# Expert weights of a mixture-of-experts layer: split whole chunks ahead of use, in a ring of three

## The chip, the cores and the metric

One core of one Trainium2 chip runs the kernel. The metric is device microseconds of one execution; lower is better. All operands in memory are fp32.

## The reference

The model is a two-layer trunk on 256 latent and 256 context tokens, width 1024: in each layer a mixer (mLSTM, neighbourhood attention, latent attention), then a feed-forward part. That of layer 0 is a dense SwiGLU, that of layer 1 sends each of the 256 latent tokens to the two best of 8 experts. The change touches only this last part:

```python
def swiglu(x, w1, w3, w2): return (silu(x @ w1) * (x @ w3)) @ w2
h = modulate(rmsnorm(x, norm2_w), shift, scale)
y = moe_ffn(h, router_w, moe_w1, moe_w3, moe_w2)   # top 2 of 8, gates from a softmax
x = x + gate * y
return rmsnorm(x, final_norm_w)
```

w1 and w3 of an expert are 1024 x 2816, w2 is 2816 x 1024: 34.6 MB for an expert, 277 MB for all eight.

## The kernel before, in words

**Places.** `stage_two` sorts the experts by how many tokens they have and works through them in that order, one *place* (`e`, 0 to 7) after another, in `experts(rank, "a")`. Which expert stands at a place is known only on the chip; the numbers are loaded into registers of the queue engine SP (line 1287) and used as offsets of the weight loads. Places 1, 3 and 5 are *narrow* (64 slots for tokens), the others *wide* (128 slots). Tokens beyond a place's slots go through a second call, `experts(rk2, "b")`, behind a branch; it is not taken here.

**Precision.** PE multiplies in fp32r, a shortened fp32 that it streams faster than fp32. To keep fp32's accuracy, an operand is split into a high part (a cast to fp32r) and a low part (the value less the high part). A wide place makes three matmuls for each weight tile (lines 1277 to 1279: high x high, high x low, low x high). A narrow place puts the high and low parts of its 64 slots side by side in 128 columns and makes two (`narrow`, lines 1078 and 1079); the rows of the low half are then added to those of the high half by a last matmul, the *fold* (line 1283), which reads a copy of the bank that ACT has made (line 1282, `aev`).

**A place.** The h phase has 11 blocks `b`, each 512 columns of the joined w1 and w3, in two chunks (`kh`) of 128 x 2048 fp32 (1 MB): 22 chunks. After each block come silu on ACT (line 1298), the multiply on DVE (line 1299, tile `as`), two transposes on PE (line 1302, `atr`), and the high and low part of the result (narrow: `agh`, lines 1309 and 1310; wide: `agh`, `agl`, lines 1314 and 1315). The y phase has 11 chunks of w2, from which two banks of 512 columns are summed, each evicted with the gate (lines 1352 and 1353, `ayy`) and scattered to the tokens (lines 1361 and 1365, `asc` and `x`); the scatter of the second half is done within the next place.

**The split.** `wsplit` (line 1048) loads a chunk on SP's queue into one of 9 raw buffers (`NQ` + `NX`; at chunks 13 and 14, `SP0`, two more buffers that are free by then), casts each 1024-column half on ACT (line 1064) and subtracts it on DVE (line 1065). The halves lie in a ring of `NSW` = 4, that is two chunks. It is called in the text where the chunk is used. In a narrow place five of the 33 chunks (`WHOLE`) are not split: PE multiplies them as fp32 (line 1076). The names in a trace: `am_0w`, `am_1w` are the raw chunks of the two `kh`, `av_0w` to `av_10w` those of w2; `wh` and `wl` are the split halves.

**The order.** Nothing writes the order of instructions out: a scheduler places what the text traces, by a model of its own, and each engine then runs its list.

**Place 0** holds extra work: `order` (line 1286) computes the sort of the experts in some 25 small DVE instructions, and `place` (line 1290) builds the marks `G` of places 1 to 7, two DVE instructions each (line 1139), all after blocks 2 and 3.

The program prints `order`, `wsplit` and the rest below. In it, `nm` is `"a"`, `P` is 128, `NF` is 22, `KT` is 8, `NFB` is 11.

Of the kernel before, what the change touches and what calls it, by code (L numbers as in the profile page):

```python
# [18 lines left out]
P = 128  # L19
D = 1024  # L20
KT = 8
# [9 lines left out]
NQ, NX = 1, 8  # L31
# [7 lines left out]
SP0 = 13  # L39
BK = 7  # L40
# [5 lines left out]
NSW = 4  # L46
# [12 lines left out]
WHOLE = (3, 10, 16, 23, 29)  # L59
T_R, T_M0, T_M1, T_UP, T_LO, T_BO, T_K = 0, 512, 896, 1280, 1408, 1536, 1664  # L60
# [10 lines left out]
def trunk(ctx: ExitStack, tc: tile.TileContext, I, out):  # L71
# [952 lines left out]
    def stage_two(s2):  # L1024
# [5 lines left out]
        nchunk = [0]  # L1030

# [7 lines left out]
        def raws(k, name):  # L1039
            if k < SP0 or k >= SP0 + len(SPEC):  # L1040
                rp, rb, rtag = (wq, NQ, "raw") if k % (NQ + NX) < NQ else (wp, NX, "rawx")
                return [rp.tile([P, 2048], F32, tag=rtag, bufs=rb, name=name)]
            where = SPEC[k - SP0]
            if where == "x1":
                return [whole.tile([P, 2048], F32, tag="x1", name=name)]
            return [wq.tile([P, 2048], F32, tag="big", name=name)]

        def wsplit(src, name, split=True):
            rt_ = raws(nchunk[0], name + "w")
            w = 2048 // len(rt_)  # L1050
            for i, raw in enumerate(rt_):
                nc.sync.dma_start(raw, src[:, i * w:i * w + w])
            nchunk[0] += 1
            if not split:
                return [(rt_[0][:, :1024], None), (rt_[0][:, 1024:], None)]
            res = []
            for j in range(2):
                h = wp.tile([P, 1024], F32R, tag="wh", bufs=NSW, name=f"{name}wh{j}")
                l = wp.tile([P, 1024], F32R, tag="wl", bufs=NSW, name=f"{name}wl{j}")
                step = 512 if nchunk[0] <= NFINE or nchunk[0] > NCHUNK - NFINE2 else 1024  # L1060
                for i in range(0, 1024, step):
                    c, o = slice(i, i + step), j * 1024 + i
                    r = rt_[o // w][:, o % w:o % w + step]
                    act.copy(h[:, c], r)  # L1064
                    dve.tensor_tensor(l[:, c], r, f32(h[:, c]), op=OP.subtract)  # L1065
                res.append((h, l))
            return res


        def unit(ws, k, c0=0, n=512):  # L1070
            return [t if t is None else t[:, k % 2 * 512 + c0:k % 2 * 512 + c0 + n] for t in ws[k // 2]]
# [93 lines left out]
        def order():  # L1165
# [4 lines left out]
            oi = tile_([P, NEXP + 1], "oi", dt=I32)  # L1170
            hot = w[:, 192:256].rearrange("p (a b) -> p a b", a=NEXP)
# [11 lines left out]
            dve.tensor_tensor(hot, pos[:, None, :].to_broadcast(sq8), row[2][:, :, None].to_broadcast(sq8), op=OP.is_equal)  # L1183
            dve.tensor_tensor(w1_, hot, i8[:, None, :].to_broadcast(sq8), op=OP.mult)
            dve.tensor_reduce(idx, w1_, AX.X, OP.add)
            dve.tensor_copy(oi[:, :NEXP], idx)
            f4 = [P, 2, NEXP, NEXP]
# [5 lines left out]
            for dst, src in ((rankp, rank), (asgp, asg), (gatep, gate)):  # L1193
                by_place(dst, src)
            dve.tensor_tensor(w1_, hot, cnt[:, None, :].to_broadcast(sq8), op=OP.mult)
# [6 lines left out]
            fold = whole.tile([P, P], F32R, tag="before", name="fold")  # L1202
            dve.tensor_copy(fold[:, :64], ident[:, 64:])
            dve.tensor_scalar(fold[:, 64:], ident[:, :64], 0.0, None, op0=OP.mult)
            return oi, fold
# [3 lines left out]
        def experts(rk, nm):  # L1209
# [3 lines left out]
            late = []  # L1213

# [43 lines left out]

            for e in range(NEXP):
# [3 lines left out]
                slim = e in thin  # L1263
                n_ = 64 if slim else P
                gts = []
                for b in range(NFB):
                    p = bank("h", 2, f"{nm}h{e}_{b}")
                    for kh in range(2):
                        ws = wsplit(weights("m13", e, b, kh), f"{nm}m{e}_{b}_{kh}", not (slim and 2 * b + kh in WHOLE))
                        for k4 in range(4):  # L1270
# [3 lines left out]
                            if slim:  # L1274
                                narrow(p, xh, (wH, wL), kt == 0, kt == KT - 1)
                                continue
# [3 lines left out]
                    if slim:  # L1280
                        ev = cp.tile([P, 512], F32, tag="pm", bufs=3, name=f"{nm}ev{e}_{b}").bitcast(F32R)
                        act.copy(ev, p)
                        pe.matmul(p, oi[1], ev, start=False, stop=True, skip_group_check=True)
                    if nm == "a" and e == 0 and b == SLB:
                        gates()
                        oi.extend(order())
                        regs.extend([0] + [nc.values_load(oi[0][0:1, s_:s_ + 1], engines=[mybir.EngineType.SP], min_val=0,
                                                          max_val=NEXP - 1) for s_ in range(1, NEXP)])
                    if nm == "a" and e == 0 and b == SLB + 1:
                        place(rankp, asgp, 1, NEXP, nm)  # L1290
                    if b == SLB + 1:
                        slots(e)
# [4 lines left out]
                    s = cp.tile([P, 512], F32, tag="pm", bufs=3, name=f"{nm}s{e}_{b}")[:n_, :256]  # L1297
                    act.activation(s, p[:n_, :256], AF.Silu)  # L1298
                    dve.tensor_tensor(s, s, p[:n_, 256:], op=OP.mult)  # L1299
                    tr = bank("t", 2, f"{nm}tr{e}_{b}")  # L1300
                    for u in range(2):
                        pe.transpose(tr[:, u * n_:(u + 1) * n_], s[:, u * P:(u + 1) * P], ident[:n_, :n_])
                    if b % 4 == 0:
                        gh4 = w1.tile([P, 8, P], F32R, tag="raw", bufs=NRAW, name=f"{nm}gh{e}_{b}")
                        gl4 = None if slim else w1.tile([P, 8, P], F32R, tag="wh", bufs=NSP, name=f"{nm}gl{e}_{b}")
                    gh = gh4[:, 2 * (b % 4):2 * (b % 4) + 2, :]
                    trv = tr[:, :2 * n_].rearrange("p (u s) -> p u s", u=2)
                    if slim:
# [10 lines left out]
                for u in range(2 * NF):  # L1319
# [3 lines left out]
                    if u % 4 == 0:  # L1323
                        ws = wsplit(weights("m2", e, u // 4), f"{nm}v{e}_{u // 4}", not (slim and 22 + u // 4 in WHOLE))
                    if e == NEXP - 1 and u == NF:
                        pm = bank("h", 2, nm + "fpm")
                        xw = cp.tile([P, KT, NL], F32, tag="h", bufs=4, name=nm + "xw")
                    if f == 0:
                        y = bank("y", 2, f"{nm}y{e}{hh}")

                    end = e == NEXP - 1 and hh == 1
                    if end and f == 0:
                        ys = [y, bank("h", 2, f"{nm}y{e}{hh}b")]
# [4 lines left out]
                    for q in range(512 // n):  # L1338
                        yq = ys[q][:, :n] if end else y
                        for u_ in units:  # L1340
                            f = u_ % NF
                            wH, wL = unit(ws, u_ % 4, q * n, n)
                            if slim:
                                narrow(yq, gts[f // 2][0][:, f % 2, :], (wH, wL), f == 0, f == NF - 1)
                                continue
# [202 lines left out]
```

## Time and profile before

| | before |
|---|---|
| median of 3 runs | 1828.65 us (1827.77 to 1829.8) |
| profiled execution | 1828.04 us |
| its span, first to last instruction | 1826.2 us |
| mean granted TensorE clock | 0.983 |
| up to the first matmul of place 0 | 1023.2 us |
| places 0 to 7 | 1023.2 to 1807.1 us |
| last scatter, final norm, output | 1807.1 to 1826.2 us |

A place is cut here at its first h matmul and its first y matmul. The eight take 108.0, 82.9, 101.5, 95.9, 101.5, 95.9, 100.6 and 97.6 us in order. Engines: PE is the matrix engine, PEld its weight loads, DVE the vector engine, ACT the scalar engine, SP the queue that issues weight loads. "ah L1079 <- DVE am_1wl L1065" reads: the instruction of line 1079 that writes tile `ah` waited for DVE's instruction of line 1065 that writes `am_1wl`. "xN" is a count of instructions. Busy times of neighbours on an engine can overlap a little, since an instruction starts before the one ahead of it has ended.

### The profile page before, as it was taken

What the parts mean: (1) busy time and instruction counts of PE and PEld (TensorE: products, weight loads), DVE (VectorE), ACT (ScalarE), POOL (GpSimd) and SP (SyncE); (2) the same over time, 40 slices, a digit from 0 to 9 for tenths busy, and PEclk for the clock granted to TensorE, in tenths of its full rate; (3) what the DMA queues carried; (4) which work ended last, traced back from release to release, by engine and by line L of the source; (5) the groups of instructions that cost most, each with busy time, mean ns of one, the idle gap of its engine ahead of it and who ended that gap; (6) DMA issues with size and microseconds to landing.
All of it is one profiled execution on the core that took longest, in us unless ns stands there. A gap on an engine that the chain in (4) does not pass through costs nothing.

```text
span 1826.2 us, 24297 instructions
## 1 busy us (share of the span) xinstructions
PE 1754.1 (96%) x8594; PEld 1333.9 (73%) x8594; DVE 1376.5 (75%) x2460; ACT 1037.5 (57%) x1661; POOL 3.0 (0%) x9
## 2 busy tenths in 40 slices
PE   6999999999999999899999899999999999999997
PEld 4776766778888888687768777678756875578886
DVE  4667757679986333577767799898968897798996
ACT  3455556533222222365466578877767776777784
POOL 0000000000000000000000000000000000000000
PEclk9999999999999999899999899999999999999998
DMA  9643211237795322331314779999989999899991
GB/s 302 230 142 127 81 45 50 74 93 239 230 324 197 93 93 84 127 101 56 104 40 161 299 279 344 398 400 361 336 323 362 382 331 337 344 395 353 338 361 46
DMA packets 82867, 410.13 MB, mean 225 GB/s; under 512 B 8912, under 2 KB 18640, under 8 KB 48944
## 3 DMA queue, kind: packets, MB, share of 16 engines
q1 hardware_dynamic: 82000, 406.62, 61.7%
q8 instruction: 70, 1.15, 0.3%
q0 software_dynamic: 304, 1.31, 0.2%
q10 hardware_dynamic: 432, 0.55, 0.1%
q14 instruction: 61, 0.50, 0.1%
HBM read 407.40 MB, written 1.05 MB: 224 GB/s over the span
## 4 chain that ended last, share of the span: by engine, by line
PE 87%; DVE 7%; ACT 3%; issue 1%; DMA 1%; SPq 0%; ACTq 0%; DVEq 0%; POOLq 0%
PE ah L1278 6%; PE ah L1277 5%; PE ah L1279 5%; DVE am_1wl L1065 2%; PE ay L1348 2%; PE ah L1079 2%; PE ay L1349 2%; PE ay L1347 2%; PE ay L1079 1%; PE ah L1078 1%; PE ah L1076 1%; PE ay L1078 1%; ACT am_1wh L1064 1%; PE ay L1076 1%; PE axgp L1224 1%
## 5 line engine op out<-in xcount | busy, mean ns | idle before, releaser
L1065 DVE TENSOR_TENSOR am_1wl<-am_1w,am_1wh 128x1024 fp32r<-128x1024 f32 (+1 forms) x172 | 203.6, 1208 | 30.4 <-ACT am_1wh L1064 29.7
L1065 DVE TENSOR_TENSOR am_0wl<-am_0w,am_0wh 128x1024 fp32r<-128x1024 f32 (+1 forms) x166 | 194.4, 1205 | 9.2 <-ACT am_0wh L1064 9.0
L1064 ACT CAST am_1wh<-am_1w 128x1024 fp32r<-128x1024 f32 (+1 forms) x172 | 172.7, 1035 | 5.4 <-PE ah L1279 2.7
L1064 ACT CAST am_0wh<-am_0w 128x1024 fp32r<-128x1024 f32 (+1 forms) x166 | 166.1, 1041 | 10.5 <-PE ah L1279 6.4
L255 DVE CUSTOM_DVE_ANT_0 junk<-awr,crow,sp 128x1024 f32<-128x1024 f32 x80 | 102.6, 1283 | 11.7 <-DMA awr<-adr 9.7
L1279 PE MATMUL ah<-am_0wh,axl 128*128 128x512 f32 x220 | 90.0, 409 | 0.0
L1278 PE MATMUL ah<-am_0wl,axh 128*128 128x512 f32 x220 | 89.3, 406 | 0.6 <-DVE am_0wl L1065 0.6
L1277 PE MATMUL ah<-am_0wh,axh 128*128 128x512 f32 x220 | 87.7, 398 | 0.0
L1278 PE MATMUL ah<-am_1wl,axh 128*128 128x512 f32 x220 | 87.3, 397 | 0.0
L1277 PE MATMUL ah<-am_1wh,axh 128*128 128x512 f32 x220 | 86.2, 392 | 0.0
L1279 PE MATMUL ah<-am_1wh,axl 128*128 128x512 f32 x220 | 85.9, 391 | 0.0
L1298 ACT ACTIVATE as<-ah 128x256 f32<-128x256 f32 (+1 forms) x88 | 33.7, 383 | 78.6 <-PE ah L1279 63.4
L1079 PE MATMUL ah<-am_1wl,axh 128*128 128x512 f32 x120 | 54.5, 454 | 10.2 <-DVE am_1wl L1065 8.2
L1299 DVE TENSOR_TENSOR as<-as,ah 128x256 f32<-128x256 f32 (+1 forms) x88 | 36.5, 414 | 27.4 <-ACT as L1298 27.1
L1278 PEld LDWEIGHTS ah<-am_0wl,axh 128*128 128x128 f32 x220 | 41.9, 191 | 10.7 <-DVE am_0wl L1065 3.0
L1078 PE MATMUL ah<-am_1wh,axh 128*128 128x512 f32 x120 | 48.6, 405 | 0.0
L1277 PEld LDWEIGHTS ah<-am_1wh,axh 128*128 128x128 f32 x220 | 41.3, 188 | 9.5
L1277 PEld LDWEIGHTS ah<-am_0wh,axh 128*128 128x128 f32 x220 | 42.0, 191 | 7.8
L1278 PEld LDWEIGHTS ah<-am_1wl,axh 128*128 128x128 f32 x220 | 41.3, 188 | 8.4 <-DVE am_1wl L1065 0.2
L1279 PEld LDWEIGHTS ah<-am_1wh,axl 128*128 128x128 f32 x220 | 41.4, 188 | 8.1
L1279 PEld LDWEIGHTS ah<-am_0wh,axl 128*128 128x128 f32 x220 | 42.0, 191 | 6.6
L1079 PE MATMUL ah<-am_0wl,axh 128*128 128x512 f32 x108 | 46.2, 428 | 0.4 <-DVE am_0wl L1065 0.3
(6197 smaller groups left out, 5107.5 us busy)
## 6 DMA issues: line engine op xcount, KB each, us to landing
am_0w<-m SPq DMA_DIRECT2D x88, 1024.0 KB, 6.7
am_1w<-m SPq DMA_DIRECT2D x88, 1024.0 KB, 7.0
awr<-adr SPq DMA_DIRECT2D x56, 512.0 KB, 4.5
aw<-ada SPq DMA_DIRECT2D x24, 512.0 KB, 4.9
aw<-ada SPq DMA_DIRECT2D x32, 256.0 KB, 6.0
av_0w<-m SPq DMA_DIRECT2D x8, 1024.0 KB, 5.4
av_1w<-m SPq DMA_DIRECT2D x8, 1024.0 KB, 6.4
av_2w<-m SPq DMA_DIRECT2D x8, 1024.0 KB, 5.0
```

Of the source, the lines that this page charges most:

```text
L255: ins = dve.tensor_tensor_reduce(out=junk, in0=w, in1=rows[v], op0=OP.mult, op1=OP.add, scale=1.0, scalar=sp[:, l, b:b + 1], accum_out=mod ...
L1064: act.copy(h[:, c], r)
L1065: dve.tensor_tensor(l[:, c], r, f32(h[:, c]), op=OP.subtract)
L1076: pe.matmul(p, f32(x), w[0], start=first, stop=last)
L1078: pe.matmul(p, x, w[0], start=first, stop=False)
L1079: pe.matmul(p, x, w[1], start=False, stop=last)
L1277: pe.matmul(p, xh, wH, start=(kt == 0), stop=False)
L1278: pe.matmul(p, xh, wL, start=False, stop=False)
L1279: pe.matmul(p, xl, wH, start=False, stop=(kt == KT - 1))
L1347: pe.matmul(yq, gh, wH, start=(f == 0), stop=False)
L1348: pe.matmul(yq, gh, wL, start=False, stop=False)
L1349: pe.matmul(yq, gl, wH, start=False, stop=(f == NF - 1))
```

## The change

1. **The split.** `load` takes the place of `wsplit`: a chunk is cast by one instruction of 2048 columns and subtracted by another (lines 1059 and 1060 of the changed kernel), into a ring of 3 whole chunks (`RING`) in place of 4 halves. The ring costs 48 KB of a partition where it was 32; in exchange the raw ring falls from 9 buffers to 7 (`NX` 8 to 6).
2. **Ahead in the text.** `need(e, c)` traces loads and splits until three split chunks, the wanted one included, are in the ring; so a split is traced up to two split chunks ahead of the matmuls that read it.
3. **Narrow places** go through `slim`: the copy of a block's bank (line 1321) follows the block's last matmul, the fold (1325), silu (1327) and multiply (1328) stand in the text half a chunk into the second next chunk, the transposes (1334) later still, and the scatter of the place before after chunk 3. `pinned` chains the instructions of PE, ACT and DVE in such a place in the order of the text, so the scheduler cannot move them.
4. **Banks.** The h and y phases share four PSUM banks (they had two each).
5. **Place 0.** `order` is cut into three parts, traced after blocks 3, 4 and 5; the marks are made two places at a time, at block 6 of each even place (`PLB`); `back` moves from block 7 to 8.

```diff
-NQ, NX = 1, 8
+NQ, NX = 1, 6
-SP0 = 13
-BK = 7
+SP0 = 10
+BK = 8
+PLB = 6
-NSW = 4
+RING = 3
...
+        def load(k, src, name, split, fine):
+            raw = raws(k, name + "w")
+            nc.sync.dma_start(raw, src)
             if not split:
...
+                return raw, None
+            h = wp.tile([P, 2048], F32R, tag="wh", bufs=RING, name=name + "wh")
+            l = wp.tile([P, 2048], F32R, tag="wl", bufs=RING, name=name + "wl")
+            step = 512 if fine else 2048
+            for i in range(0, 2048, step):
+                c = slice(i, i + step)
+                act.copy(h[:, c], raw[:, c])
+                dve.tensor_tensor(l[:, c], raw[:, c], f32(h[:, c]), op=OP.subtract)
+            return h, l
...
+            def need(e, c):
+                k = e * NCH + c
+                while nxt[0] < NCHUNK and sum(map(splits, range(k, nxt[0] + 1))) <= RING:
+                    j = nxt[0]
...
+                    ready[j] = load(k0 + j, weights(*src), ...)
+                    nxt[0] += 1
+                return ready.pop(k)
...
+        def pinned(traced, n):
+            last = {}
+            for i in traced[n:]:
+                if i.engine in (mybir.EngineType.PE, mybir.EngineType.Activation, mybir.EngineType.DVE):
+                    if i.engine in last:
+                        tc.add_manual_dep(i, last[i.engine].name, ..., reason="in order")
+                    last[i.engine] = i
...
+            def slim(e, xg, o, late):
...
+                if late:
+                    at(3, 1, late.pop())
+                at(7, 0, lambda: slots(e))
+                at(15, 0, lambda: back(e))
+                for c in range(NCH):
+                    ws = need(e, c)
...
+                            narrow(p, xg[0][:, kt, o:o + P], unit(ws, k), kt == 0, kt == KT - 1)
+                            if kt == KT - 1:
+                                copy_out(b)
+                                at(c + 1, 1, lambda b=b: add_low(b))
+                                at(c + 3, 0, lambda b=b: turn(b))
...
+                if e in thin:
+                    traced = nc.cur_bb.bb.instructions
+                    n = len(traced)
+                    slim(e, xg, o, late)
+                    pinned(traced, n)
+                    continue
...
-                    p = bank("h", 2, f"{nm}h{e}_{b}")
+                    p = bank("h", 4, f"{nm}h{e}_{b}")
...
-                        y = bank("y", 2, f"{nm}y{e}{hh}")
+                        y = bank("h", 4, f"{nm}y{e}{hh}")
...
+                        if SLB < b <= SLB + 3:
+                            oi[:] = [next(steps)]
+                    if nm == "a" and e % 2 == 0 and b == PLB:
+                        place(rankp, asgp, e + 1, min(e + 3, NEXP), nm)
```

**PE, start of the narrow place 3, the kernel before.** `ah3_0` and `ah3_1` are the banks of blocks 0 and 1, `am3_1_0wh0` is the high part of a half chunk of block 1, `aev3_0` the copy, `atr3_0` the transposes of block 0:

```order
L1079 MATMUL ah3_0_11399<-am3_0_1wl1_11425,axh3_11164 128x512
L1078 MATMUL ah3_1_11448<-am3_1_0wh0_11451,axh3_11164 128x512
L1283 MATMUL ah3_0_11399<-aev3_0_11436,fold_8895 128x512
L1079 MATMUL ah3_1_11448<-am3_1_0wl0_11452,axh3_11164 128x512
L1078 MATMUL ah3_1_11448<-am3_1_0wh0_11451,axh3_11164 128x512
L1079 MATMUL ah3_1_11448<-am3_1_0wl0_11452,axh3_11164 128x512
L1078 MATMUL ah3_1_11448<-am3_1_0wh1_11455,axh3_11164 128x512
L1079 MATMUL ah3_1_11448<-am3_1_0wl1_11456,axh3_11164 128x512
L1078 MATMUL ah3_1_11448<-am3_1_0wh1_11455,axh3_11164 128x512
L1302 MATMUL atr3_0_11442<-ck_58,as3_0_11439 128x64 x2
```

The same place of the changed kernel, from the last matmuls of chunk 2 (`am3_2`) on:

```order
L1072 MATMUL ah3_1_11072<-am3_2wh_11035,axh3_10826 128x512
L1073 MATMUL ah3_1_11072<-am3_2wl_11036,axh3_10826 128x512
L1325 MATMUL ah3_0_11041<-aev3_0_11064,fold_8908 128x512
L1070 MATMUL ah3_1_11072<-am3_3w_11039,axh3_10826 128x512 x4
L1290 MATMUL asc24_11097<-GT_8639,ayy2_10752 128x256 x4
L1290 MATMUL asc26_11104<-GT_8639,ayy2_10752 128x256 x4
L1072 MATMUL ah3_2_11111<-am3_4wh_11052,axh3_10826 128x512
L1073 MATMUL ah3_2_11111<-am3_4wl_11053,axh3_10826 128x512
L1072 MATMUL ah3_2_11111<-am3_4wh_11052,axh3_10826 128x512
L1073 MATMUL ah3_2_11111<-am3_4wl_11053,axh3_10826 128x512
L1334 MATMUL atr3_0_11116<-ck_58,as3_0_11082 128x64 x2
```

The fold of block 0 stood one matmul behind the block's last; now all eight matmuls of chunk 2 are between them. The transposes stood seven matmuls after the fold; now an unsplit chunk, the scatter and half of chunk 4 are between.

**ACT, the same place, before:** casts of raw chunks (`am3_b_kh`, halves `wh0` and `wh1`), the copy, silu and the high part of block 0.

```order
L1064 CAST am3_1_0wh0_11451<-am3_1_0w_11449 128x1024
L1064 CAST am3_1_0wh1_11455<-am3_1_0w_11449 128x1024
L1282 CAST aev3_0_11436<-ah3_0_11399 128x512
L1298 ACTIVATE as3_0_11439<-ah3_0_11399 64x256
L1309 CAST agh3_0_11445<-atr3_0_11442 128x2x64
L1064 CAST am3_2_0wh0_11501<-am3_2_0w_11499 128x1024
L1064 CAST am3_2_0wh1_11505<-am3_2_0w_11499 128x1024
L1282 CAST aev3_1_11473<-ah3_1_11448 128x512
L1298 ACTIVATE as3_1_11490<-ah3_1_11448 64x256
L1064 CAST am3_2_1wh0_11519<-am3_2_1w_11517 128x1024
```

ACT, changed:

```order
L1059 CAST am3_2wh_11035<-am3_2w_11033 128x2048
L1059 CAST am3_4wh_11052<-am3_4w_11050 128x2048
L1321 CAST aev3_0_11064<-ah3_0_11041 128x512
L1059 CAST am3_5wh_11068<-am3_5w_11066 128x2048
L1327 ACTIVATE as3_0_11082<-ah3_0_11041 64x256
L1059 CAST am3_6wh_11087<-am3_6w_11085 128x2048
L1321 CAST aev3_1_11095<-ah3_1_11072 128x512
L1339 CAST agh3_0_11119<-atr3_0_11116 128x2x64
L1327 ACTIVATE as3_1_11127<-ah3_1_11072 64x256
L1059 CAST am3_7wh_11132<-am3_7w_11130 128x2048
```

The copy, silu and high part of block 0 stood together between two casts; now a whole cast stands between copy and silu, and another between silu and the high part. (Chunk 3 is one of those that are not split.)

**DVE, place 0, blocks 4 to 6 of the changed kernel** (before, all of these and the marks stood in one row between the second half of chunk 7 and chunk 8):

```order
L1060 TENSOR_TENSOR am0_13wl_9073<-am0_13w_9070,am0_13wh_9072 128x2048
L1190 TENSOR_REDUCE rt_8613<-ordw_8906 128x16
L1195 TENSOR_TENSOR ordw_8906<-ordw_8906 128x64
L1189 TENSOR_TENSOR ordw_8906<-ordw_8906,rt_8613 128x128
L1196 TENSOR_REDUCE ordw_8906<-ordw_8906 128x8
L1190 TENSOR_REDUCE rt_8613<-ordw_8906 128x16
L1197 TENSOR_TENSOR ordw_8906<-ordw_8906,ck_58 128x8
L1201 TENSOR_TENSOR rt_8613<-rt_8613,ck_58 128x16
L1414 TENSOR_TENSOR as0_5_9097<-as0_5_9097,ah0_5_9051 128x256
L1198 TENSOR_REDUCE ordw_8906<-ordw_8906 128x1
L1060 TENSOR_TENSOR am0_14wl_9109<-am0_14w_9106,am0_14wh_9108 128x2048
```

A few small instructions of the sort (`ordw`) now stand between one subtraction and the next. The 14 marks of places 1 to 7, traced in places 0, 2, 4 and 6, are all placed by the scheduler within place 0: five at the end of its h phase, nine in its y phase.

## Rows read from the trace of the kernel before

**Rows 1.** The page, busy time of the engines, share of the span, instructions.

```profile
PE 1754.1 (96%) x8594; PEld 1333.9 (73%) x8594; DVE 1376.5 (75%) x2460; ACT 1037.5 (57%) x1661; POOL 3.0 (0%) x9
```

**Rows 2.** Windows: e0, e1, e3 (h, y), e4 (h): length, busy times, clock, DMA share, GB/s.

```profile
core 0: us, PE busy (x) PEld busy (x) DVE busy (x) ACT busy (x) POOL busy (x), PEclk, DMA share, GB/s
1023.20:1097.30 74.10, 72.20 (x323) 58.75 (x324) 65.03 (x108) 54.22 (x71) 0.00 (x0) 0.94 0.69 261
1097.30:1131.20 33.90, 33.90 (x159) 27.77 (x158) 32.47 (x46) 27.06 (x33) 0.00 (x0) 1.00 0.91 334
1131.20:1186.90 55.70, 55.32 (x221) 37.02 (x220) 50.25 (x62) 47.00 (x69) 0.00 (x0) 1.00 0.98 395
1186.90:1214.10 27.20, 26.72 (x100) 17.47 (x99) 24.30 (x28) 19.18 (x23) 0.00 (x0) 1.00 0.96 386
...
1315.60:1384.20 68.60, 62.83 (x222) 36.00 (x220) 51.23 (x63) 48.93 (x70) 0.00 (x0) 1.00 0.89 337
1384.20:1411.50 27.30, 26.80 (x101) 17.63 (x99) 24.10 (x27) 19.18 (x22) 0.00 (x0) 1.00 0.92 358
1411.50:1478.00 66.50, 66.50 (x315) 54.68 (x314) 60.41 (x71) 49.60 (x66) 0.00 (x0) 1.00 0.97 377
```

**Rows 3.** Waits in e5 (1513 to 1609 us): us in total, times, longest.

```profile
PEld ah L1079 <- DVE am_1wl L1065: 12.1, 20, 1.0
DVE as L1299 <- ACT as L1298: 10.6, 10, 3.1
```

**Rows 4.** The chain of waits within e5, in order of time: start us, us, what.

```profile
1532.39 0.51 PE ah L1283
...
1533.21 1.04 ACT am_1wh L1064
1534.28 1.23 DVE am_1wl L1065
...
1538.59 0.46 PE ah L1283
```

**Rows 5.** Subtractions and casts, whole span: duration ns min/median/max; forms of 512 and 1024 columns.

```profile
L1065 DVE TENSOR_TENSOR am_0wl<-am_0w,am_0wh x166: 683/1218/1229, 994.1 to 1768.6; 128x1024 fp32r<-128x1024 f32 x162, 128x512 fp32r<-128x512 f32 x4
...
L1064 ACT CAST am_0wh<-am_0w x166: 617/1051/1065, 993.4 to 1766.9; 128x1024 fp32r<-128x1024 f32 x162, 128x512 fp32r<-128x512 f32 x4
```

**Rows 6.** DVE's timeline around the end of e5: start us, us, line, operation, count.

```profile
1599.73 0.86 DVE L1365 SCALAR_TENSOR_TENSOR x<-asc,modT,x 128x256 f32<-128x256 f32 x2
...
1602.78 2.35 DVE L1065 TENSOR_TENSOR av_9wl<-av_9w,av_9wh 128x1024 fp32r<-128x1024 f32 x2
...
1609.84 0.74 DVE L1353 SCALAR_TENSOR_TENSOR ayy<-ay,gslot,ayy 128x512 fp32r<-128x512 f32 x1
```

**Rows 7.** Groups in e5: count, busy us, mean ns, idle time before, releaser.

```profile
L1282 ACT CAST aev<-ah 128x512 fp32r<-128x512 f32 x11 | 6.5, 587 | 11.1 <-PE ah L1079 9.4 <-PE ah L1076 1.7
...
L1299 DVE TENSOR_TENSOR as<-as,ah 64x256 f32<-64x256 f32 x11 | 4.5, 412 | 10.6 <-ACT as L1298 10.6
L1298 ACT ACTIVATE as<-ah 64x256 f32<-64x256 f32 x11 | 4.2, 378 | 6.5 <-PE ah L1283 6.5
...
L1310 DVE TENSOR_TENSOR agh<-atr,agh 128x128 fp32r<-128x128 f32 x11 | 3.1, 285 | 1.6 <-ACT agh L1309 1.6
...
L1309 ACT CAST agh<-atr 128x128 fp32r<-128x128 f32 x11 | 2.9, 265 | 3.8 <-PE atr L1302 3.0
```

**Rows 8.** Waits in e1 (1131.2 to 1214.1 us).

```profile
DVE am_1wl L1065 <- ACT am_1wh L1064: 3.2, 4, 1.5
```

**Rows 9.** Window in the middle of e1, columns as in rows 2.

```profile
1150.00:1200.00 50.00, 49.62 (x192) 32.09 (x190) 43.82 (x52) 40.00 (x59) 0.00 (x0) 1.00 0.99 404
```

**Rows 10.** DVE's timeline in place 0.

```profile
1052.49 3.16 DVE L1139 TENSOR_SCALAR G<-ck,rt 128x128 fp32r<-128x128 f32 x12
...
1055.96 1.22 DVE L1065 TENSOR_TENSOR am_0wl<-am_0w,am_0wh 128x1024 fp32r<-128x1024 f32 x1
```

**Rows 11.** Window of place 0, columns as in rows 2.

```profile
1052.00:1060.00 8.00, 6.10 (x35) 4.88 (x35) 8.00 (x24) 2.56 (x4) 0.00 (x0) 1.00 0.49 147
```

More of the change, by code (lines that the diff above doesn't have):

```diff
@@ L1041, in raws @@
                 rp, rb, rtag = (wq, NQ, "raw") if k % (NQ + NX) < NQ else (wp, NX, "rawx")
-                return [rp.tile([P, 2048], F32, tag=rtag, bufs=rb, name=name)]
+                return rp.tile([P, 2048], F32, tag=rtag, bufs=rb, name=name)
             where = SPEC[k - SP0]
             if where == "x1":
[L1045 to L1053, printed above, removed]
-            if not split:
[L1055 to L1067, printed above, removed]
@@ L1170, in order @@
             oi = tile_([P, NEXP + 1], "oi", dt=I32)
+            fold = whole.tile([P, P], F32R, tag="before", name="fold")
+            out_ = oi, fold
             hot = w[:, 192:256].rearrange("p (a b) -> p a b", a=NEXP)
@@ L1186, in order @@
             dve.tensor_copy(oi[:, :NEXP], idx)
+            regs.extend([0] + [nc.values_load(oi[0:1, s_:s_ + 1], engines=[mybir.EngineType.SP], min_val=0,
+                                              max_val=NEXP - 1) for s_ in range(1, NEXP)])
             f4 = [P, 2, NEXP, NEXP]
@@ L1201, in order @@
             dve.tensor_tensor(rk2, rankp, row[3][:, None, :].to_broadcast([P, 2, NEXP]), op=OP.subtract)
-            fold = whole.tile([P, P], F32R, tag="before", name="fold")
             dve.tensor_copy(fold[:, :64], ident[:, 64:])
             dve.tensor_scalar(fold[:, 64:], ident[:, :64], 0.0, None, op0=OP.mult)
-            return oi, fold
+            yield out_
+        def pinned(traced, n):
[3 more added lines that the diff above has]
+                    if i.engine in last:
+                        tc.add_manual_dep(i, last[i.engine].name, mybir.DependencyInfo(
+                            mybir.DependencyClass.NoSync, mybir.DependencyReason.DATA), reason="in order")
+                    last[i.engine] = i
         oi, regs = [], []
@@ L1279, in experts @@
                             pe.matmul(p, xl, wH, start=False, stop=(kt == KT - 1))
[L1280 to L1291, printed above, removed]
+                    if nm == "a" and e == 0:
+                        if b == SLB:
+                            gates()
+                            steps = order()
+                        if SLB < b <= SLB + 3:
+                            oi[:] = [next(steps)]
+                    if nm == "a" and e % 2 == 0 and b == PLB:
+                        place(rankp, asgp, e + 1, min(e + 3, NEXP), nm)
+                    if b == PLB:
                         slots(e)
```

151 lines of the change are left out of this document (99 added, 52 removed).

## Prediction

> **What bounds the kernel now.** I began with the busy times of the whole span [rows 1]. TensorE (PE) is busy for 96% of it, which looks as if only fewer matmuls could help. That share is an average over stages, so the next view is the span cut at the first matmul of each half of a place [rows 2]. Everything before 1023 us is untouched by the diff; the eight places lie between 1023.2 and 1807.1 us. Three kinds show. In a wide place (e4, 128 slots, three matmuls per weight tile) PE is busy for all of the 66.5 us of its first half: it is the bound there. In the narrow places e3 and e5 (64 slots, two matmuls per tile) PE is busy for 62.83 of 68.6 us, though it has a third less to do, and VectorE (DVE) for only 51.23 and ScalarE (ACT) for 48.93: nobody is full, so they wait for each other in turn. The narrow place e1 has the same instructions and takes 55.7 + 27.2 = 82.9 us where e3 takes 68.6 + 27.3 = 95.9. So 13 us of e3 are neither work nor data, and e5 repeats e3.
>
> The waits of e5 say who waits [rows 3]: PE's weight loads for the low half of the weights (DVE `wl`, line 1065) 12.1 us, DVE's multiply for ACT's silu 10.6 us. The chain of waits gives them an order [rows 4]: the fold matmul (line 1283), the cast of a 1024-column half on ACT, its subtraction on DVE, the matmuls, the next fold. It is a loop with one turn for each of the 11 blocks b of a place, 6.2 us from fold to fold (11 × 6.2 is the 68 us), because in ACT's order the casts of later halves stand behind a copy and a silu that wait for PE.
>
> **The change part by part.**
>
> *Casts and subtractions of 2048 columns.* A 512-column subtraction takes 0.683 us and a 1024-column one 1.218, so 512 more cost 0.535, and one of 2048 is by estimate 1.218 + 2 × 0.535 = 2.29 us. For ACT, 0.617 and 1.051 give 1.92 [rows 5]. Two subtractions back to back take 2.35 from the first start to the last end, so the second starts 0.085 before the first ends [rows 6]; at that rate a chunk costs 2 × (1.218 − 0.085) = 2.27 now and 2.29 − 0.085 = 2.20 then, a gain of 0.07 us. The bounds are 0 and 2 × 1.218 − 2.29 = 0.15; I take 0.07, from the back-to-back row, since that is how DVE runs in the narrow places. In the wide ones PE covers it and the gain is nothing. The Trainium skill ("VectorE: DVE Perf Modes", "The TRN2 errata — SBUF-src ops pay a fixed extra latency per instruction") gives an fp32 tensor_tensor (N + 151)/0.96 ns, so 2.29 us for 2048 columns; if that is paid without overlap, the three narrow places cost 3 × 28 × 0.085 = 7 us more than I sum below. The single durations here agree with it, the back-to-back row does not.
>
> *Narrow places: whole chunks traced ahead, text order kept, the fold one chunk later, transposes two.* This takes the loop apart. The casts of the next split chunks now stand ahead of the copy of block b, and the fold, silu and multiply come when other matmuls are there to cover them. What is late next is DVE. Its bill for a narrow place: 28 split chunks × 2.20 = 61.6; 11 blocks × (0.41 multiply + 0.285 low half − 2 × 0.085) = 5.8; scatter, 8 × 0.43 = 3.4; two evictions × 0.74 = 1.5 [rows 6, 7]. Sum 72.3 us. ACT stays below: 28 × 1.92 + 11 × (0.587 + 0.378 + 0.265) = 67.3 [rows 7]. A ring of three asks for no more: a slot that comes free needs a cast and a subtraction, 1.92 + 2.29 = 4.2, before it is used again two chunks later, and two split chunks cost DVE more than that, 4.4 and its small work. How much idle time remains is the unknown. Below it is 0 (72.3). Above it is what e1 shows, the narrow place that e3's loop does not hold: DVE busy for 50.25 + 24.30 of 82.9 us, so 8.35 idle (80.65). In e1, 3.2 us of DVE's idle time is a second half's subtraction that waits for its cast [rows 8]; with casts traced ahead I take half of it off, 1.6, and stay near that row: 6.75 idle, **79 us a narrow place**. e1 gains 82.9 − 79 = 3.9, e3 and e5 16.9 each: 37.7 us.
>
> *Data.* A place is 33 chunks of 1.049 MB, 34.6 MB. In the middle of e1 the queues are busy for 0.99 of the time and move 404 GB/s [rows 9]; at that, 79 us bring 31.9 MB. The other 2.7 MB, 2.6 chunks, must lie loaded when the place begins, and the raw ring falls from 9 buffers to 7. A wide place takes a chunk in 66.5/22 = 3.0 us and the queues bring one in 2.6, so the ring is full then, and of seven buffers I count one or two in the split and one or two in flight: about four are loaded. It is enough, with little to spare. I cost it at nothing; if that cover is gone, the first rival has the price.
>
> *Wide places.* After the last matmul of a block the freed slot needs, in the new order, a silu of about 0.38, a cast of 1.92, a subtraction of 2.29 and some 0.4 of small DVE work, 5.0 us, and PE has two chunks, 66.5/11 = 6.05 us, before it wants it. Cover 1.05 us: cost nothing. The gain is nothing as well, for PE is the bound.
>
> *Place 0, the ordering steps spread, the marks G moved later.* Now a burst of small DVE work, among it 12 marks in 3.16 us, holds up a subtraction until 1055.96, and PE is idle for 1.9 of the 8 us there [rows 10, 11]. That goes. Of the 14 marks, nine land in the second half of place 0, where DVE is busy for 32.47 of 33.9 us; 9 × 3.16/12 = 2.4 us overrun it by up to 1.0 [rows 2]. Bounds −1.9 and +1.0; I take −1.0, nearer to the idle time that the trace shows, since that idle time is measured and the overrun is only possible. The loads of the experts' numbers into SP's registers move from block 2 to block 4 of place 0, past the issues of some four chunks; the first chunk that needs one is wanted near 1131 us, so nothing. The scatter of the expert before is now pinned after chunk 3 of a narrow place: behind it on PE stands chunk 4, and its operands come from an eviction that is four chunks old; nothing, and at most that eviction's 0.74 us a place [rows 6] if it came late. The four shared banks, the tail: nothing, since no wait in the rows above is one for a bank.
>
> Sum: −37.7 − 1.0 = −38.7 us on the profiled execution's 1828.04, 1789.3. The median of the runs shown, 1828.65, is 0.6 above it: **1790 us**.
>
> **The rivals.**
>
> *The queues become the bound (chance 0.21).* With no reserve a narrow place takes 34.6/404 = 85.7 us. For it: seven raws, and e1 already at 0.98 of the queues' time [rows 2]. Against it: a wide place leaves the queues 3.0 us for a chunk that they bring in 2.6, so no narrow place begins with nothing in store. e1 +2.8, e3 and e5 −10.2 each, place 0 −1: **1810 us**. The Trainium skill ("Perfetto Trace Analysis", "Engine Utilization") puts a core's share of the memory at 358 GB/s where both cores of a pair read and 435 as the ceiling of one alone; by the first, a narrow place would take 96.7 us and the kernel 1843. The row of 404 speaks for the second, and I give the first 0.01, on the slower side.
>
> *DVE runs dry of waits (0.13).* The narrow places reach its bill of 72.3 us: e1 −10.6, e3 and e5 −23.6 each, −57.8 − 1: **1770 us**. For it: nothing in the new order makes DVE wait on PE. Against it: 72.3 us bring only 29.2 MB, so more than five chunks would have to be in store.
>
> *The wide places stall on the coarser ring (0.11, slower).* A slot of 2048 columns is free only when all 12 matmuls of its chunk are done, and its cast and subtraction cannot begin on the first half alone. If one more subtraction (2.29) stands ahead of the one that is wanted, 5.0 becomes 7.3 against 6.05: 1.25 us for each of 11 blocks in five wide places, +69: **about 1858 us**. It turns the sign from 38.7/55 = 0.70 us a block on. For it: DVE is busy for 60.41 of 66.5 us in a wide half [rows 2]. Against it: the same row, PE does not wait there now, and DVE keeps 6 us in hand.
>
> *The loop stays (0.04).* The pinned order makes ACT wait at the copy as before and the narrow places keep their times: within 0.2% of 1828.
>
> **How the numbers follow.** The forecast as told, 1776 to 1802, gets 0.50, the likeliest; the others 0.21, 0.13, 0.11 and 0.04, and 0.01 the queues at half the memory. The range of 8 in 10 reaches from just under DVE's bill to a little over the queues' bound: **1766 to 1816**; out of it are the slower cases (0.12), the loop (0.04) and a rest of some 0.04 at the ends. A measurement of this kernel tells a change from none at about 0.2%, 3.7 us: faster 0.84, same 0.04, slower 0.12.
>
> **What would show it right or wrong.** Right: e1, e3 and e5 alike, 76 to 82 us each; the wide halves at 66 to 67; in e5 the waits of PE for `wl` fewer and the fold's chain gone, DVE busy for 88% or more of a narrow place; one subtraction of 2048 columns at about 2.29 us. The queues' rival shows as casts that wait for a DMA in the second half of a narrow place and at over 0.97 of queue time. The slower rival shows as PE idle in e4 before a `wl` load, 1 us a block. The forecast is wrong if e3 and e5 still differ from e1, or if a wide half moves by more than 2 us.

## The result and the profile after

The changed kernel takes 1805.41 us (median of 4 runs, 1804.62 to 1806.02) against 1829.22 us of the kernel before on the same chip: a ratio of 0.9871, 95% interval 0.9854 to 0.9888. The time falls by 23.8 us. The forecast was 38.7 us less, 1790; the range, 1766 to 1816, holds the result.

The profiled execution took 1805.85 us, with a span of 1804.0. Cut at the first matmul of each half of a place, with the columns of rows 2, it reads (place e0, then the narrow places e1, e3 and e5 and the h phase of the wide e4; h, then y):

```profile
1026.60:1096.70 70.10, 70.10 (x314) 57.77 (x314) 58.97 (x78) 49.52 (x49) 0.00 (x0) 0.94 0.71 266
1096.70:1131.80 35.10, 35.10 (x170) 28.96 (x169) 33.51 (x43) 25.29 (x22) 0.00 (x0) 1.00 0.92 335
1131.80:1188.20 56.40, 55.04 (x220) 36.98 (x218) 48.21 (x42) 45.26 (x50) 0.00 (x0) 1.00 0.96 371
1188.20:1216.10 27.90, 26.76 (x102) 17.70 (x101) 23.43 (x20) 19.06 (x15) 0.00 (x0) 1.00 1.00 411
...
1317.10:1373.50 56.40, 55.03 (x219) 36.97 (x218) 48.17 (x42) 45.23 (x50) 0.00 (x0) 1.00 1.00 390
1373.50:1401.50 28.00, 26.88 (x103) 17.71 (x101) 23.53 (x20) 19.05 (x15) 0.00 (x0) 1.00 1.00 415
1401.50:1468.40 66.90, 66.77 (x316) 54.71 (x315) 58.79 (x49) 47.23 (x44) 0.00 (x0) 1.00 0.96 362
...
1502.50:1558.90 56.40, 55.03 (x219) 36.96 (x218) 48.16 (x42) 45.24 (x50) 0.00 (x0) 1.00 0.95 381
1558.90:1586.90 28.00, 26.88 (x103) 17.70 (x101) 23.52 (x20) 19.02 (x15) 0.00 (x0) 1.00 1.01 413
```

The three narrow places are now alike, 84.3, 84.4 and 84.4 us, where rows 2 had 82.9, 95.9 and 95.9. e3 and e5 have lost 11.5 us each; e1, which the old loop did not hold, is 1.4 longer. PE has become almost full in them, 55.03 of 56.4 us in the h phase of e3, where it was 62.83 of 68.6.

| us | e0 | e1 | e2 | e3 | e4 | e5 | e6 | e7 | all eight |
|---|---|---|---|---|---|---|---|---|---|
| before | 108.0 | 82.9 | 101.5 | 95.9 | 101.5 | 95.9 | 100.6 | 97.6 | 783.9 |
| after | 105.2 | 84.3 | 101.0 | 84.4 | 101.0 | 84.4 | 100.8 | 97.3 | 758.4 |

That is 25.5 us less. Place 0 begins 3.4 us later in this execution (1026.6 and not 1023.2), and the tail is unchanged, which gives, to rounding, the 22.2 us by which the span is shorter.

In e5 the waits that led rows 3 are gone or small. What is left, by the view of the waits of e5 (us in total, times, longest), is single waits of DVE for a cast, at chunks 14, 20 and 27 of e5, 7 a little less, and chunk 0 of the next place:

```profile
DVE am_20wl L1060 <- ACT am_20wh L1059: 2.9, 1, 2.9
DVE am_14wl L1060 <- ACT am_14wh L1059: 2.6, 1, 2.6
DVE av_27wl L1060 <- ACT av_27wh L1059: 2.2, 1, 2.2
DVE am_0wl L1060 <- ACT am_0wh L1059: 2.2, 1, 2.2
...
DVE am_7wl L1060 <- ACT am_7wh L1059: 1.4, 1, 1.4
```

Each is the fourth chunk behind an unsplit one (3, 10, 16, 23, 29). Three timelines show chunk 14. PE first (start us, us, line, operation, count), around the unsplit chunk 10, whose first half is a like piece some 2 us earlier, and at the first low part of chunk 14:

```profile
1529.99 1.98 PE L1070 MATMUL ah<-am_10w,axh 128*128 128x512 f32 x4
1531.41 0.79 PE L1325 MATMUL ah<-aev,fold 128*128 128x512 f32 x1
1532.04 0.39 PE L1072 MATMUL ah<-am_11wh,axh 128*128 128x512 f32 x1
...
1533.64 0.39 PE L1073 MATMUL ah<-am_11wl,axh 128*128 128x512 f32 x1
...
1538.84 0.50 PE L1073 MATMUL ah<-am_14wl,axh 128*128 128x512 f32 x1 [0.18 <-DVE am_14wl L1060]
```

Then ACT and DVE in the same stretch:

```profile
1528.67 1.90 ACT L1059 CAST am_13wh<-am_13w 128x2048 fp32r<-128x2048 f32 x1
1530.47 0.26 ACT L1339 CAST agh<-atr 128x128 fp32r<-128x128 f32 x1
1532.24 0.38 ACT L1327 ACTIVATE as<-ah 64x256 f32<-64x256 f32 x1 [1.50 <-PE ah L1325]
1534.07 0.59 ACT L1321 CAST aev<-ah 128x512 fp32r<-128x512 f32 x1 [1.45 <-PE ah L1073]
1534.55 1.91 ACT L1059 CAST am_14wh<-am_14w 128x2048 fp32r<-128x2048 f32 x1
```

```profile
1531.06 2.28 DVE L1060 TENSOR_TENSOR am_13wl<-am_13w,am_13wh 128x2048 fp32r<-128x2048 f32 x1
...
1533.46 0.40 DVE L1328 TENSOR_TENSOR as<-as,ah 64x256 f32<-64x256 f32 x1
1536.49 2.29 DVE L1060 TENSOR_TENSOR am_14wl<-am_14w,am_14wh 128x2048 fp32r<-128x2048 f32 x1 [2.63 <-ACT am_14wh L1059]
```

While PE works on the unsplit chunk, the three slots of the ring hold chunks 11, 12 and 13. Chunk 14 needs the slot of 11, and its cast stands in the kept order behind the copy of the block that ends with chunk 11. Both wait for the last matmul of chunk 11, which starts at 1533.64. ACT is done with 13 at 1530.57 and DVE with everything at 1533.86; then the cast takes 1.91, and DVE stands until 1536.49. The unsplit chunk holds PE for 3.43 us (eight records of 0.43; the trace has two for each of its four matmuls), where a split one takes 8 × 0.23 = 1.84. The five waits shown add up to 11.3 us of DVE's idle time in e5. PE waits far less, at chunk 14 for 0.18 us. What that makes of the 12.7 us in which DVE is idle in e5 is worked out below.

### The profile page after: what moved, and what is told of

Read it like the earlier page. It is cut to its first block, busy times and chain, and to the rows that moved or that the text cites. A ratio compares the mean times of both kernels' runs of the same rounds, so it can differ in the third digit from the quotient of the medians.

```text
span 1804.0 us, 23626 instructions
## 1 busy us (share of the span) xinstructions
PE 1739.2 (96%) x8594; PEld 1338.9 (74%) x8594; DVE 1351.3 (75%) x2214; ACT 1007.4 (56%) x1415; POOL 3.0 (0%) x9
## 3 DMA queue, kind: packets, MB, share of 16 engines
HBM read 407.40 MB, written 1.05 MB: 226 GB/s over the span
## 4 chain that ended last, share of the span: by engine, by line
PE 88%; DVE 6%; ACT 2%; DMA 2%; issue 1%; SPq 0%; ACTq 0%; DVEq 0%
PE ah L1396 6%; PE ah L1397 6%; PE ah L1395 6%; PE ay L1455 3%; PE ay L1454 3%; PE ay L1456 3%; PE ah L1073 2%; PE ah L1070 2%; PE ah L1072 2%; PE axgp L1250 1%; PE ay L1070 1%; PE asc L1290 1%; PE ay L1072 1%; PE ay L1073 1%; PE cq L93 1%
## 5 line engine op out<-in xcount | busy, mean ns | idle before, releaser
L1423 ACT CAST agh<-atr 128x256 fp32r<-128x256 f32 x55 | 20.5, 372 | 75.7 <-PE atr L1417 75.4
L1294 DVE SCALAR_TENSOR_TENSOR x<-asc,modT,x 128x256 f32<-128x256 f32 x64 | 27.0, 475 | 5.5 <-PE asc L1290 5.5
L1413 ACT ACTIVATE as<-ah 128x256 f32<-128x256 f32 x55 | 21.1, 384 | 9.8 <-PE ah L1397 9.7
L1321 ACT CAST aev<-ah 128x512 fp32r<-128x512 f32 x33 | 19.1, 580 | 13.3 <-PE ah L1073 9.5
L1060 DVE TENSOR_TENSOR am_20wl<-am_20w,am_20wh 128x2048 fp32r<-128x2048 f32 x8 | 18.3, 2293 | 9.1 <-ACT am_20wh L1059 9.1
L277 PE MATMUL ada<-aw,sc 128*32 128x128 f32 x256 | 12.7, 317 | 12.2 <-DMA aw<-ada 12.0
L1060 DVE TENSOR_TENSOR am_0wl<-am_0w,am_0wh 128x2048 fp32r<-128x2048 f32 (+1 forms) x11 | 18.5, 1706 | 7.3 <-ACT am_0wh L1059 7.2
L1424 DVE TENSOR_TENSOR agl<-atr,agh 128x256 fp32r<-128x256 f32 x55 | 23.0, 418 | 0.8 <-ACT agh L1423 0.8
L1290 PE MATMUL asc<-GT,ayy 128*128 128x256 f32 x128 | 20.7, 294 | 2.8 <-DVE ayy L1310 2.5
L1414 DVE TENSOR_TENSOR as<-as,ah 128x256 f32<-128x256 f32 x55 | 22.8, 414 | 0.0
L1417 PE MATMUL atr<-ck,as 128*128 128x128 f32 x110 | 20.9, 271 | 0.0
```

The lines of the kernel that those rows point to most:

```text
L1060: dve.tensor_tensor(l[:, c], raw[:, c], f32(h[:, c]), op=OP.subtract)
L1290: pe.matmul(p[:, u * NL:(u + 1) * NL], yy[:, j, (d2 + u) * P:(d2 + u + 1) * P], GT[:, e, :], start=(j == 0), stop=(j == 1))
```

## The experiments

The runs are called by their labels, run e1 to run e11; e0 to e7 without the word run are places, as before. Two theories were set against each other. A: the ring of three whole chunks sets the pace of the narrow places, through the waits behind their unsplit chunks. B: the queues do, which the windows above show busy for 0.95 to 1.01 of the time; and the result lies nearer to that rival's 1810 us than to the forecast's 1790.

**Run e1, half the bytes.** Each load brings 1024 columns, which every reader uses twice; the product is another, the instructions and their sizes are the same.

```diff
-            nc.sync.dma_start(raw, src)
+            nc.sync.dma_start(raw[:, :1024], src[:, :1024])
...
+            r = raw[:, None, :1024].to_broadcast([P, 2, 1024])
```

> Each chunk's load brings only its first 1024 columns and every reader uses them twice, so the arithmetic is another but each engine runs the same instructions on the same sizes; the queues move half the bytes. Theory A (the ring of three): a place e1, e3 or e5 stays at 83 to 84.5 us, since ACT and DVE wait after each unsplit chunk for a slot of the ring, and the kernel at 1801 to 1805. Theory B (the queues, 0.95 to 1.01 busy in the narrow places of the changed kernel, set their pace): a narrow place falls to about 79, the kernel to about 1789.

Measured: 1802.42 us. Place e5, h and y:

```profile
1497.10:1553.60 56.50, 55.12 (x219) 37.02 (x219) 48.25 (x42) 45.26 (x50) 0.00 (x0) 1.00 0.59 199
1553.60:1581.60 28.00, 26.88 (x103) 17.70 (x101) 23.51 (x20) 18.98 (x16) 0.00 (x0) 1.00 0.60 205
```

With the queues at 0.6 and 200 GB/s, places e1, e3 and e5 take 84.3, 84.4 and 84.4 us, to the tenth what they took. The queues do not set their pace. B falls.

**Run e2, a ring of four, five raw buffers.**

```diff
-RING = 3
+RING = 4
-NQ, NX = 1, 6
+NQ, NX = 1, 4
```

> A ring of four whole chunks, paid for with two raw buffers (7 to 5). Theory A: one more subtraction fits beside each of the five unsplit chunks of a narrow place, some 2 us each, so narrow places of 77 to 81 and a kernel of 1785 to 1797. Theory B: with less in store a narrow place is no shorter than 34.6 MB at 404 GB/s, 85.7, and the kernel at or above 1809.

Measured: 1836.31 us, slower than the kernel before (ratio 1.0047, 1.0027 to 1.0067). The narrow places take 91.9, 93.9 and 98.0 us, and in place e5 casts wait for their data 14 times, 17.0 us in all. The longest of these waits, and the place's two halves:

```profile
ACT av_30wh L1059 <- DMA av_30w<-m: 3.6, 1, 3.6
1517.90:1581.40 63.50, 57.60 (x219) 39.00 (x218) 49.70 (x43) 46.19 (x51) 0.00 (x0) 0.95 0.92 364
1581.40:1615.90 34.50, 28.49 (x103) 19.20 (x102) 24.64 (x20) 20.77 (x15) 0.00 (x0) 0.90 0.91 356
```

So with five raw buffers the data do become the bound, and by more than the 85.7 us that I had worked out, since loads that wait for a free buffer leave the queues at 0.92 and 0.91. The granted clock adds to it: 0.95 and 0.90 here, 1.00 in the changed kernel; how much of the 98.0 us it makes was not parted. What a deeper ring would give by itself, this run cannot show.

**Run e3, the ring of before under the new order.** Halves of 1024, four of them, nine raw buffers.

```diff
-RING = 3
+RING = 2
-NQ, NX = 1, 6
+NQ, NX = 1, 8
-SP0 = 10
+SP0 = 13
...
-            h = wp.tile([P, 2048], F32R, tag="wh", bufs=RING, name=name + "wh")
+                h = wp.tile([P, 1024], F32R, tag="wh", bufs=2 * RING, name=f"{name}wh{j}")
```

> The changed kernel with the ring of before: halves of 1024, four of them, nine raw buffers. New are only the order, the banks and place 0. Theory A: the shorter ring makes the waits after unsplit chunks longer, narrow places 86 to 90, kernel 1810 to 1820. Theory B: with nine raws the queues run ahead again and a narrow place takes 80 to 82, kernel 1793 to 1799. If the order alone is the change, 84.4 and 1805.

Measured: 1808.57 us, narrow places 85.6, 86.7 and 86.7: the shorter ring costs 1.3 to 2.3 us a place, at theory A's lower bound and a little under it. Of the 11.5 us that places e3 and e5 have gained, 9.2 come with the order and what goes with it (splits traced ahead, the shared banks, place 0), without the new ring.

**Runs e4 and e7, halves.** Run e4 casts, subtracts and frees the three chunks of the ring by halves; run e7 casts and subtracts by halves but keeps slots of a whole chunk.

```diff
-            step = 512 if fine else 2048
+            step = 512 if fine else 1024
```

(the edit of run e7; run e4 is the edit of run e3 with a ring of 3, `NX` 6 and `SP0` 10)

> The changed kernel's memory (three chunks in the ring, seven raws) but cast, subtracted and freed by halves of 1024. Theory A: a slot comes free half a chunk, 0.9 us of PE, earlier after each unsplit chunk: 5 x 0.9 less 28 x 0.07 of DVE, narrow places 81 to 82.5, kernel about 1798. If the size of an instruction is what counts, 28 x 0.07 = 2 us more a narrow place, kernel about 1811. Theory B: no difference, 1805.

> The changed kernel with casts and subtractions of 1024 columns, but slots of the ring still whole chunks. It parts the two things that the ring of six halves changed. If the gain there came from slots that come free by halves, this gives nothing or loses 28 x 0.07 = 2 us a narrow place: 84.4 to 86.4, kernel 1805 to 1811. If it came from the first half's low part being ready after 1.05 + 1.22 us and not after 1.92 + 2.29, 1.9 us earlier at four or five places behind an unsplit chunk, narrow places take 77 to 82 and the kernel 1790 to 1799.

Measured: run e4 1795.28 us, narrow places 80.7, 81.5 and 82.9; run e7 1794.20 us, narrow places 81.4, 82.2 and 82.4. Both beat the changed kernel by some 10 us (ratios to before 0.9822 and 0.9805), 7 to 8 of them in the narrow places. Since run e7 has the whole gain with whole slots, the slots are not what matters: the delay of the first half is. A cast of 1024 and its subtraction are done 1.05 + 1.22 = 2.27 us after a slot comes free, one of 2048 after 1.92 + 2.29 = 4.2, and PE can begin on the first half.

**Runs e10 and e11, five halved chunks.** Halves only where the cast waits behind an unsplit chunk; run e11 adds a spare raw buffer for chunk 16.

```diff
-            step = 512 if fine else 2048
+            step = 512 if fine else 1024 if k < NCHUNK and (k - 4) // NCH in NARROW and (k - 4) % NCH in WHOLE else 2048
```

> The changed kernel with only five chunks of each narrow place cast and subtracted by halves, the ones whose cast waits for a slot behind an unsplit chunk (chunks 7, 14, 20, 27 and the next place's 0). If the gain of the halves comes from there, nearly all of it comes back: narrow places 81.5 to 82.7, the kernel 1796 to 1800. If it comes from every chunk, less than a quarter: 83.8 to 84.4, 1803 to 1805.

> The five halved chunks and chunk 16 loaded into the spare buffer. If waiting for data takes up to 1 us at the end of a narrow place, 1 us less a place than with the five alone, the kernel 1793 to 1797; if not, the same as the five alone.

Measured: run e10 1801.99 us, narrow places 83.5, 83.5 and 84.6; run e11 1798.16 us, 83.5, 83.6 and 83.5. I had expected nearly all of run e7's gain; in places e1 and e3 some 0.9 of 2.2 to 2.9 us came back. The times from one chunk's first matmul to the next chunk's say why: in place e3 of run e10 the 1.57 us that PE lost at chunks 7, 14, 20 and 27 are gone, and it loses 0.75 us more than before at chunks 8, 15, 21, 22 and 28 behind them, which are still cast whole. So the delay counts at those as well. In place e5 of run e10 the cast of chunk 30 waits 1.4 us for its data; the spare buffer takes away the 1.1 us by which that place is longer than e3, and nothing in the places that did not wait so.

**Run e6, without the kept order.**

```diff
-                    pinned(traced, n)
```

> The changed kernel without the chain that keeps the narrow places in the order of the text: the scheduler places the fold, the silu and the transposes early again, as it did before. If the kept order is what ended the loop of e3 and e5, they go back to 90 to 96 us each and the kernel to 1817 to 1829. If tracing the splits ahead and the ring of three do it alone, they stay at 84 to 86 and the kernel at 1805 to 1808.

Measured: 1835.71 us, ratio 1.0039 (1.0028 to 1.0049): slower than the kernel before. Places e3 and e5 take 95.9 us each, e1 89.5. That e3 and e5 come to what they took before to the tenth is in part chance, for the granted clock in the first half of e5 is 0.97 here and was 1.00 before; and the profiled execution, 1831.5 us, is the fastest of eight. The chain within e5 has its loop back (start us, us, what):

```profile
1528.91 2.30 DVE am_5wl L1060
1531.25 0.50 PE ah L1073
...
1533.66 1.91 ACT am_7wh L1059
1535.60 2.30 DVE am_7wl L1060
1537.95 0.50 PE ah L1073
...
1540.34 1.92 ACT am_9wh L1059
1542.28 2.30 DVE am_9wl L1060
```

From one subtraction to the next but one are 6.69 us (1528.91 to 1535.60), a block's time; rows 4 had 6.2. Nothing overlaps in it: a cast of 1.91, a subtraction of 2.30, the matmuls, the copy of the block. The kept order is what ends the loop; the larger ring and splits traced ahead do not by themselves.

**Run e9, every chunk split.**

```diff
-WHOLE = (3, 10, 16, 23, 29)
+WHOLE = ()
```

> The changed kernel with no unsplit chunk in the narrow places: DVE's bill by the prediction's rows is 33 x 2.20 + 10.7 = 83.3 us a place, PE's is 1.6 x 5 = 8 less. If DVE's 12.7 idle us of a narrow place stand behind its unsplit chunks, they go, and a narrow place takes 84 to 87 us with DVE busy for 96% or more, the kernel 1804 to 1813. If they are spread over all chunks, about 95 us a place and 1837.

Measured: 1798.97 us, narrow places 82.5 each, shorter than with five unsplit chunks. Place e5:

```profile
1499.10:1553.90 54.80, 52.25 (x219) 36.23 (x218) 54.38 (x45) 50.31 (x53) 0.00 (x0) 1.00 0.99 398
1553.90:1581.70 27.80, 25.25 (x103) 17.20 (x102) 27.80 (x22) 22.71 (x17) 0.00 (x0) 1.00 1.01 419
```

DVE is busy for 54.38 + 27.80 = 82.18 of 82.6 us. Its bill has grown by 10.5 us (from 71.68) and its idle time has fallen from 12.7 to 0.4. Without unsplit chunks DVE's work alone sets the pace. The unsplit chunks take 10.5 us of work from DVE and give PE 5 × (3.43 − 1.84) = 8.0 us; with them a place is 1.9 us longer in this order.

**Run e5, the third chunk of place 0 held back.** The cast and subtraction of chunk 2 are issued behind the gather of place 0.

```diff
+                with tc.issue_after(tail[0].ins) if k == 2 else ExitStack():
+                    act.copy(h[:, c], raw[:, c])
+                with tc.issue_after(tail[1].ins) if k == 2 else ExitStack():
+                    dve.tensor_tensor(l[:, c], raw[:, c], f32(h[:, c]), op=OP.subtract)
```

> One thing of the changed kernel altered: the cast and the subtraction of chunk 2 of place 0 are issued only behind the gather of place 0. In the changed kernel they stand ahead of the last steps of layer 1's norm and router on ACT and DVE, and place 0 begins at 1026.6 us where it began at 1023.2. If that is the cause of the late start, place 0 begins at 1023 to 1024 and the kernel takes 1802 to 1803. If the order of PE at the end of the layer is the cause, the start stays at 1026.6 and the kernel at 1805.

Measured: 1802.32 us (1800.79 to 1805.45). The median is what the first case said, but the profiled execution, the slowest of the four, begins place 0 at 1025.4, with every place as in the changed kernel but e0 (105.4) and e1 (84.9); that holding chunk 2 back gains anything is not shown. My cause falls: with chunk 2 as early as in the changed kernel, place 0 begins at 1023.1 in run e6, 1022.6 in run e1, 1021.8 in run e11 and 1027.2 in run e9. By PE's 5000th instruction, before chunk 2's subtraction, the profile after was already 3.4 us behind (995.1 and 991.7). Part of this goes with the granted clock: between 910 and 917 us it is 0.76 in the changed kernel and in run e9 and 1.00 in runs e6 and e11, and from PE's 4300th to its 4600th instruction the first two take 51.8 us, the others 50.2 to 50.3. Why the clock differs there, and the rest of the scatter, stay open.

**Run e8, the best.** Six halves, chunk 2 held back, chunk 16 in the spare buffer.

```diff
+            if k < NCHUNK and k // NCH in NARROW and c == 16:
+                return wq.tile([P, 2048], F32, tag="big", name=name)
```

> The ring of six halves, with chunk 2 of place 0 issued late and chunk 16 of the narrow places loaded into the buffer that holds the expert's result later on, which is free in the h phase. From 1795.3: the start 2 us earlier, and in each narrow place up to 1 us of waiting for data at its end gone: 1790 to 1793. If the start is not to be had, 1793 to 1795.

Measured: 1791.41 us, ratio 0.9782 (0.9765 to 0.9800), the fastest of all. Narrow places 79.9, 81.5 and 81.5. It begins place 0 at 1025.9, so the gain is not in the start. Place e5:

```profile
1493.90:1549.20 55.30, 54.54 (x220) 37.32 (x219) 50.12 (x62) 47.60 (x71) 0.00 (x0) 1.00 1.00 406
1549.20:1575.40 26.20, 26.01 (x102) 17.97 (x101) 25.75 (x31) 19.86 (x24) 0.00 (x0) 1.00 0.99 399
```

PE is busy for 80.55 of 81.5 us, and the queues for 0.99 to 1.00. The next gain would have to come from less work for PE; whether the queues could then follow was not tried.

## Why the prediction was right or wrong

**The loop of e3 and e5, right.** It was a loop in the order, not work or data, and keeping the text's order ends it: run e6 has 95.9 us without the order, run e3 86.7 with the order and the ring of before. All three narrow places became alike, as forecast, but at 84.3 to 84.4 us and not at 76 to 82; DVE is busy for 85% of them and not for 88%. (The fold stands behind the last matmul of the next chunk, as the order list shows, not half a chunk into the second next one, as item 3 of the change has it.)

**The price of a chunk, right, but the wrong price to ask for.** One subtraction of 2048 columns takes 2.28 to 2.29 us and the next begins 2.21 after it, against 2.29 and 2.20 worked out:

```profile
1507.38 2.29 DVE L1060 TENSOR_TENSOR am_4wl<-am_4w,am_4wh 128x2048 fp32r<-128x2048 f32 x1
1509.59 2.29 DVE L1060 TENSOR_TENSOR am_5wl<-am_5w,am_5wh 128x2048 fp32r<-128x2048 f32 x1
```

The Trainium skill ("Vector Engine (DVE) Microarchitecture Reference", "5.2 Measured stream behaviour on trn2 (trn3 not measured)") gives 1.0417 ns a column and some 75 ns for an instruction after overlap, measured on 32-bit integer streams; by estimate that is 2.21 us for 2048 columns. The trace agrees, and the 7 us that the rule cited in the prediction would have added without overlap are not there. What the step left out is delay: run e7 goes back to halves, pays DVE's 0.07 us a chunk again and wins 2.0 to 2.9 us a narrow place, because the first half is ready 1.9 us sooner.

**DVE's bill, right; its idle time, wrong.** The bill was 72.3 us and measures 48.16 + 23.52 = 71.68 in e5. The idle time was put at 6.75 us, between 0 and 8.35, and measures 84.4 − 71.7 = 12.7, outside its bounds. This term of the sum was mis-sized, and it failed at two steps, both about the five unsplit chunks.

The first is "What is late next is DVE". PE's own work has no bill in the sum. The order of PE's instructions is the same in the changed kernel and in the nine runs that keep it and the five unsplit chunks. If each of the 33 chunks is given the shortest time that any narrow place of these kernels shows from its first matmul to the next chunk's, PE needs 79.5 us for a place (an estimate from the traces, a little high if a chunk waits everywhere). The forecast of 79 us left PE no wait at all, and the 72.3 us of the rival in which DVE never waits were out of reach. Rows 2 could have warned: PE is busy for 55.32 + 26.72 = 82.0 of e1's 82.9 us, and nothing in the change takes matmuls from it. So 79.5 − 71.7 = 7.8 us of DVE's idle time are PE's longer work.

The second is "A ring of three asks for no more". It compared a slot's 4.2 us with DVE's time for two split chunks and forgot the unsplit ones, whose 3.43 us of PE no term priced: in that time no slot comes free. The casts after them come late, and PE waits in turn: 84.4 − 79.5 = 4.9 us a place. In e5 nearly all of it stands at or just behind the chunks listed with the waits above: 1.3 us at chunk 2, 1.05 at 28, 0.35 to 0.5 each at 14, 20, 22 and 27, less at 7, 9, 15 and 21. Run e9 bears both out: without unsplit chunks PE has 8.0 us less to do, DVE's bill of 82.2 us is the larger one, and 0.4 us of its idle time is left. The upper bound was no bound either, for e1's 8.35 us were idle time of another ring and order; e1 lost 1.4 us and did not gain 3.9. In sum the narrow places gave 21.6 us (11.5 + 11.5 − 1.4) where 37.7 were forecast.

**Data, right for seven buffers, with less to spare than said.** Run e1 shows that they cost nothing in the narrow places, run e2 that two buffers fewer, beside a ring of four, make each 8 to 14 us longer. The time measured lies outside the 1776 to 1802 us of the forecast as told, inside the wide range, and next to the 1810 of the rival with the queues as the bound, with queue shares to match. It was still not the queues: here they were busy for 0.95 to 1.01 of the narrow places and held up nothing, since half the bytes left the places as long as they were. That the range holds the result owes more to its width than to the sum.

**Wide places, right.** 101.0 us for 101.5; the slower rival is out, for PE is busy for 66.77 of 66.9 us in a wide half.

**Place 0, mis-sized.** −2.8 us for −1.0. The h phase lost 4.0 with the burst that held up the subtraction: from chunk 8's first matmul to chunk 9's it was 8.4 us before and is 2.7 now, more than the 1.9 us of PE's idle time that the sum went by. The y phase, in which nine marks stand, is 1.2 us longer (35.1 for 33.9), just over their bound of 1.0.

## What to carry to other kernels

Add up the work of every engine before one is called the next bound: here PE's 79.5 us stood above DVE's 72.3, and only DVE's was summed. When engines pass buffers around in a ring, work out for each kind of step how long every engine needs it, the rare kinds too: a step that spares one engine work can still stop it, if it holds another engine while no buffer comes free. A larger instruction saves a fixed cost and adds delay before the first consumer can start; on a path that waits for a slot the delay was the larger of the two here, 1.9 us for 0.07. And a bound taken from another version's idle time holds only as long as ring and order are the same.

## What the runs showed of the hardware that was not expected

An unsplit fp32 matmul of 512 columns shows as two records in the trace, 0.43 us apart, so its chunk holds PE for 3.43 us, where the four matmuls that the order counts suggest 1.72. One core alone drew 419 to 420 GB/s over the 27 to 28 us of a y phase (runs e9 and e4), more than the 404 of rows 9. And the stages ahead of place 0 vary by about 5 us from profile to profile (place 0 begins between 1021.8 and 1027.2 us), as much as several of the effects studied here, in part with the granted clock (0.76 to 1.00 between 910 and 917 us). The three narrow places of the changed kernel, and those of run e9, agree within 0.1 us, so they were the better measure.
